# A hybrid decoder layer on one core: room of the output passes, issuer of the last stores, order of the last pair

## The chip, the cores and the metric

One core of a Trainium2 chip runs the whole layer in one launch. The metric is the device time of one execution in microseconds (us). Timed three times, the kernel before took 1909.26 us in the median (1907.34 to 1910.01). The engines are named as the profile names them: PE is TensorE (matmul), PEld its weight load, DVE is VectorE, ACT is ScalarE, POOL is GpSimd, and SP is the engine that issues DMA transfers; SPq is its queue.

## The reference

The layer has 2048 tokens of 1024 features, all float32. Cut to what matters:

```python
u = rmsnorm(h, norm_mix);  z = u @ w_in                    # 1024 -> 5392
aq, ak, av, gq, gk, gv, g_low, za, zg = split(z)
y_att = swa_sink_attention(rope(aq), rope(ak), av, sinks)  # 16 heads, window 128
log_g = log_sigmoid(g_low @ w_gate_up + b_gate) / 16
y_gla = rmsnorm(gla_chunked(gq, gk, gv, log_g), gla_norm)  # 4 heads
y = concat([y_att * silu(za), y_gla * silu(zg)]) @ w_out   # 2048 -> 1024
h = h + y
gate = sigmoid(rmsnorm(h, ple_norm) @ w_ple_gate)          # 1024 -> 1024
h = h + gate * (p @ w_ple_proj)                            # 256 -> 1024
out = rmsnorm(h, final_norm)
```

## The kernel before

Every float32 product is taken as three matmuls: each operand is split into a rounded part h (ScalarE copies it to float32r) and a rest l (VectorE or GpSimd subtracts), and hh + hl + lh are summed in PSUM.

**Phase 1** computes the input projection and both groups of heads, in two halves of eight token tiles. `uth` and `utl` hold the normed input of a half, transposed. `load_w` (L265 to L294) brings columns of w_in through `raw` tiles, splits them into wh and wl in one of two weight slots, and keeps the split form in DRAM for the second half. The results go to the DRAM tensors `yts`, one per token tile: features 0 to 7 by the attention tiles (L480), 8 to 15 by the four gated heads (`gla_tile`, store at L587). In the second half the generator `right_operands` also prepares the right-hand matrices of the output passes and stores them to DRAM (`td`). The key and value buffers and the raw tiles (`kvp`, `rawp`) lie at the right end of SBUF; they are closed before the gate weights of the last gated head are loaded, and the first three prepared matrices are loaded into their place (`tpr`).

**Phase 2** is three passes: pass 0 and 1 multiply the two halves of y by w_out and add the residual, pass 2 is the gate with w_ple_gate. Each works on pairs of token tiles, in blocks of one or two pairs: (0,1), (2), (3), (4), (5), (6,7), and in pass 2 (0,1), (2) to (7). A pair's 256 by 1024 times 1024 by 1024 product is formed by seven products of quarter blocks, by sums and differences of blocks (`combos` makes the left operands C, `T[i]` are the right ones). The seven are taken in ORDER = (0, 4, 1, 6, 5, 2, 3); each is 12 matmuls of 512 columns (`prod`, L774 to L776). Products 1, 2 and 3 add onto the PSUM banks of 0, 4 and 6, and `after` says what is done with each result. In pass 0 and 1 the quarters of the result are summed into the residual tiles q11 to q22; `norm_pair` then squares and scales them, and its transposes run in the next block (`posts`).

In pass 2 (`gate_block`) each quarter passes through `gated`: sigmoid, times the projection of p (`proj`, four groups of six matmuls, on w_ple_proj loaded by `load_wq`), plus the residual hr, and a square for the final norm; `finish` scales and stores to `out`. `load_p` brings a tile of p, transposes and splits it. For the last pair, product 3 is done in two halves of 256 columns (`halves`), and each of the other steps follows it.

**What sets the order.** The code is written in program order, but the order on each engine is laid down when the kernel is built, by a scheduler that simulates the instructions with estimated costs: of those that can run, the one that stands first in the program goes first. On the chip each engine then works strictly in that order; SP also issues its transfers in order, and each waits for its inputs and for a free buffer. Tiles with one tag share `bufs` buffers; a tile waits until its buffer's former tile has been read. With `reuse_waits="tile"` a tile of a new pool waits only for the older tiles at its own addresses.

The pools of phase 2 are laid from the left in the order in which they are opened: `xpb` (17 x2 tiles of 2 KiB, 8 C tiles of 4 KiB, 10 x2b tiles of 2 KiB), `tpb` (4 matrices of 16 KiB), `fs`. They lie over the weight slots (34 KiB), uth and utl (64), c1 and wk of phase 1. The weights of w_ple_proj (8 tiles) and of final_norm (2) are x2b tiles, of which the residuals of passes 0 and 1 (eight for a block of two pairs) also are. The gate pass takes its q tiles, p tiles and hr tiles from x2.

Of the kernel before, what the change touches and what calls it, by code (L numbers as in the profile page):

```python
# [38 lines left out]
def hybrid_block_kernel(  # L39
# [57 lines left out]
    def x2(name, shape=(P, 4, P), dtype=F32):  # L97
        return p2p["xpb"].tile(list(shape), dtype, name=name, tag="x2", bufs=17)
# [27 lines left out]
    with ExitStack() as p1:  # L126
        kvs = p1.enter_context(ExitStack())
        kvp = kvs.enter_context(tc.tile_pool(name="kvp", bufs=1, side="right"))
        rawp = kvs.enter_context(tc.tile_pool(name="rawp", bufs=9, side="right"))
# [39 lines left out]
        def constants():  # L169
# [33 lines left out]

            pos_f = wk.tile([16, P], F32, name="pos_f", tag="w1", bufs=8)
# [60 lines left out]
        def load_w(cols, fast=False):  # L265
# [9 lines left out]
            for k0 in range(0, KD, 2):  # L275
                ks_ = slice(k0, k0 + 2)
# [4 lines left out]
                raw = rawp.tile([P, 2, SW], F32, name="raw", tag="raw")  # L281
# [4 lines left out]
                act.activation(wh[:, ks_, 0:n], raw[:, :, 0:n], AF.Copy)  # L286
                eng = dve if fast and k0 % 4 == 0 else pool
                eng.tensor_tensor(wl[:, ks_, 0:n], raw[:, :, 0:n], wh[:, ks_, 0:n], op=ALU.subtract)  # L288
# [260 lines left out]
        def gla_tile(half, h, wz, lt, ops):  # L549
# [37 lines left out]
            pace[0] = nc.sync.dma_start(yts[t][:, 8 + 2 * h:10 + 2 * h, :], oy).ins  # L587
# [9 lines left out]
        def right_operands():  # L597
            units = [(ps_, k, c) for ps_ in range(3) for k in range(4) for c in range(4)]

            def piece(name, dtype=F32):  # L600
                return rawp.tile([P, 2 * SW], dtype, name=name, tag="raw")[:, 0:512].rearrange("p (b n) -> p b n", b=4)
# [54 lines left out]
        for half in range(2):  # L656
# [4 lines left out]
            for s_ in range(HT + LAG):  # L661
# [5 lines left out]
                if s_ < HT:  # L667
                    a = section_a(half, s_, wA)
                    next(a)
                    if half == 0 and s_ == 0:  # L670
                        constants()
                    tick()
# [11 lines left out]
            for i in range(4):  # L684
# [9 lines left out]
                if half == 1 and i == 3:  # L694
# [50 lines left out]
    with ExitStack() as p2:  # L745
        for name in ("xpb", "tpb", "fs"):
            p2p[name] = p2.enter_context(tc.tile_pool(name=name, bufs=1, reuse_waits="tile"))
        fs = p2p["fs"]
        load_T(0, ORDER[3:], T)


        def combos(As):
            Cs = [[None] * 7 for _ in As]
            ss = [x2("s1") for _ in As]
            for i in ORDER:
                for C, (a11, a12, a21, a22), s_ in zip(Cs, As, ss):
# [9 lines left out]
                    C[i] = p2p["xpb"].tile([P, 2, 4, P], F32R, name=f"c{i}", tag="c", bufs=8)  # L766
# [13 lines left out]
        def products(Cs, T, after, last=None):  # L780
            banks = [{} for _ in Cs]
            two = len(Cs) > 1
            for i in ORDER:
# [111 lines left out]
        def load_p(t):  # L895
            pi = x2("pi", (P, DPLE))
# [19 lines left out]
        def gate_block(prs, Cs, T, posts):  # L916
            two = len(prs) > 1
            last = prs[-1] == NP - 1
            qs = [[x2(f"q{i}", (P, 512)) for i in range(4)] for _ in prs]
# [11 lines left out]
            def finish(n, i, s2):  # L931
# [20 lines left out]
            def after(i, n, ps):  # L952
# [5 lines left out]
                elif i == 1:  # L958
                    act.activation(q11, ps, AF.Copy)
                elif i == 6:  # L960
                    add(dve, q22, q22, ps)
                elif i == 5:
                    add(dve, q21, q21, ps)
                    add(dve, q22, q22, q21)
                elif i == 2:
                    add(dve, q12, q21, ps)
                    s2 = sums()
                    pps = proj(pTs[n, 0], banks())
                    gated(n, 0, 0, pps, s2)
                    gated(n, 0, 1, pps, s2)  # L970
                    if last:
                        state["s"] = s2
                        state["p"] = proj(pTs[n, 1], [pt("t"), pt("t")])
                        state["s1"] = sums()
                        gated(n, 1, 1, state["p"], state["s1"])
                    else:
# [113 lines left out]
```

## Time and profile before

| | us |
|---|---|
| median of three runs (lowest, highest) | 1909.26 (1907.34, 1910.01) |
| the profiled execution | 1904.04 |
| its span, first to last instruction | 1902.3 |
| busy: TensorE matmul, weight load | 1814.7, 1612.9 |
| busy: VectorE, ScalarE, GpSimd | 1203.3, 961.1, 699.3 |

The span is what the profile shows of the profiled execution; 1.7 us lie around it. Busy times are sums over the span, so they say which engine could be the bound, and the windows say where. A matmul's start is measured and its end modelled, so the pace of TensorE is read from the distance of starts. The granted clock is given as a share of full speed: 1.0 is 2.4 GHz, 0.5 is 1.2 GHz. In a wait, the name behind the arrow is what ended it last.

### The profile page before, as it was taken

The numbers are of one execution on the slowest core, as the hardware profiler recorded it, in microseconds if no ns is written. First come the engines' busy times: TensorE is split into PE (matmuls) and PEld (weight loads), VectorE is DVE, ScalarE is ACT, GpSimd is POOL, SyncE is SP. The second block draws the span as 40 slices with busy tenths as digits, with TensorE's granted clock in tenths as the row PEclk, the third lists the DMA queues.
The fourth block names the chain that finished last, engine by engine and source line by source line (L and its number), as shares of the span: only waits on it lengthen the run. The fifth ranks groups of instructions, "written<-read, shape, count | busy, mean of one in ns | idle before, by whom it ended". The sixth has DMA issues, their size and how long they took to land. (4 is left out here: it accounts for less than half of the span.)

```text
span 1902.3 us, 32715 instructions
## 1 busy us (share of the span) xinstructions
PE 1814.7 (95%) x11297; PEld 1612.9 (85%) x11297; DVE 1203.3 (63%) x2663; ACT 961.1 (51%) x2598; POOL 699.3 (37%) x916
## 2 busy tenths in 40 slices
PE   6999999999999999999999999999899999998997
PEld 6989898998898889898888988988788888787886
DVE  6454785466556474578766756574667667665864
ACT  5544666465557464456654655563422244453543
POOL 5442554534526362544455445352200010102432
PEclk9999999999999999999999999999999999999998
DMA  8332442415324352655576566565685966884542
GB/s 281 122 101 81 147 136 92 155 53 170 97 66 143 102 180 90 199 146 174 178 205 206 163 195 182 160 195 192 230 281 194 324 237 219 313 309 151 179 139 83
DMA packets 326741, 326.78 MB, mean 172 GB/s; under 512 B 23137, under 2 KB 259825, under 8 KB 326321
## 3 DMA queue, kind: packets, MB, share of 16 engines
q1 hardware_dynamic: 326576, 324.70, 52.5%
q8 instruction: 89, 1.46, 0.3%
q14 instruction: 76, 0.61, 0.1%
HBM read 186.08 MB, written 138.54 MB: 171 GB/s over the span
## 5 line engine op out<-in xcount | busy, mean ns | idle before, releaser
L85 PE MATMUL acc<-wh,uth 128*128 128x256 f32 (+1 forms) x1664 | 476.8, 287 | 14.5 <-DVE m L563 4.5
L86 PE MATMUL acc<-wl,uth 128*128 128x256 f32 (+1 forms) x1664 | 472.6, 284 | 6.2 <-DMA wl<-wd 6.0
L87 PE MATMUL acc<-wh,utl 128*128 128x256 f32 (+1 forms) x1664 | 471.1, 283 | 0.0
L85 PEld LDWEIGHTS acc<-wh,uth 128*128 128x128 f32 x1664 | 316.0, 190 | 25.6 <-ACT v L522 5.9
L86 PEld LDWEIGHTS acc<-wl,uth 128*128 128x128 f32 x1664 | 315.7, 190 | 12.9 <-DMA wl<-wd 8.6
L87 PEld LDWEIGHTS acc<-wh,utl 128*128 128x128 f32 x1664 | 315.7, 190 | 2.0
L460 POOL TENSOR_TENSOR pq<-pq,pmask 128x512 fp32r<-128x512 f32 x128 | 178.2, 1408 | 292.9 <-ACT pq L67 285.8
L85 PE MATMUL acc<-uth,wh 128*128 128x512 f32 x512 | 204.3, 399 | 4.8 <-DVE m L563 3.8
L87 PE MATMUL acc<-uth,wl 128*128 128x512 f32 x512 | 201.7, 394 | 0.3 <-DMA wl<-wd 0.3
L86 PE MATMUL acc<-utl,wh 128*128 128x512 f32 x512 | 201.9, 394 | 0.0
L774 PE MATMUL acc<-T,c 128*128 128x512 f32 (+1 forms) x344 | 135.5, 395 | 6.7 <-ACT u L829 6.3
L775 PE MATMUL acc<-T,c 128*128 128x512 f32 (+1 forms) x344 | 135.1, 393 | 0.0
L776 PE MATMUL acc<-T,c 128*128 128x512 f32 (+1 forms) x344 | 135.0, 393 | 0.0
L446 ACT ACTIVATE s<-s,sm 128x128 f32<-128x128 f32 x256 | 99.7, 391 | 51.1 <-DVE sm L442 51.1
L85 PEld LDWEIGHTS acc<-uth,wh 128*128 128x128 f32 x512 | 96.4, 188 | 26.8 <-DVE m L563 5.2
L859 POOL TENSOR_TENSOR ssh<-ssh 128x1 f32<-128x1 f32 x16 | 3.3, 205 | 313.8 <-ACT junk L858 313.8
L288 POOL TENSOR_TENSOR wl<-raw,wh 128x512 fp32r<-128x512 f32 (+1 forms) x82 | 109.6, 1367 | 20.0 <-ACT wh L286 10.2
L87 PEld LDWEIGHTS acc<-uth,wl 128*128 128x128 f32 x512 | 96.1, 188 | 22.5 <-DMA wl<-wd 0.7
L86 PEld LDWEIGHTS acc<-utl,wh 128*128 128x128 f32 x512 | 96.2, 188 | 18.7
L67 ACT ACTIVATE c<-s 128x512 fp32r<-128x512 f32 x72 | 45.1, 629 | 111.1 <-DVE s L104 32.4
L774 PE MATMUL o<-T,c 128*128 128x512 f32 (+1 forms) x252 | 99.3, 394 | 0.0
L775 PE MATMUL o<-T,c 128*128 128x512 f32 (+1 forms) x252 | 98.6, 391 | 0.0
(289 smaller groups left out, 4409.7 us busy)
## 6 DMA issues: line engine op xcount, KB each, us to landing
T<-td SPq DMA_DIRECT2D x84, 512.0 KB, 9.4
wd<-wh SPq DMA_DIRECT2D x20, 1024.0 KB, 5.6
wd<-wl SPq DMA_DIRECT2D x20, 1024.0 KB, 6.3
wh<-wd SPq DMA_DIRECT2D x80, 256.0 KB, 5.4
wl<-wd SPq DMA_DIRECT2D x80, 256.0 KB, 5.5
raw<-in_w_in SPq DMA_DIRECT2D x68, 256.0 KB, 5.6
y<-yts SPq DMA_DIRECT2D x64, 256.0 KB, 5.6
td<-th SPq DMA_DIRECT2D x48, 256.0 KB, 2.8
```

The source lines that it names most:

```text
L67: act.activation(h, src, AF.Copy)
L85: pe.matmul(ps, lhs_h(k), rhs_h(k), start=(k == 0), stop=False)
L86: pe.matmul(ps, lhs_h(k), rhs_l(k), start=False, stop=False)
L87: pe.matmul(ps, lhs_l(k), rhs_h(k), start=False, stop=(k == nk - 1))
L288: eng.tensor_tensor(wl[:, ks_, 0:n], raw[:, :, 0:n], wh[:, ks_, 0:n], op=ALU.subtract)
L446: act.activation(s[:, j, :], s[:, j, :], AF.Exp, bias=ng[:, j:j + 1], accum_out=su[:, j:j + 1])
L460: pool.tensor_tensor(pq[:, 2 + i, :].rearrange("p (h n) -> p h n", h=4), pq[:, i, :].rearrange("p (h n) -> p h n", h=4), pmb, op=ALU.mult)
L774: pe.matmul(ps, c[:, 0, k, :], t[:, 0, k, sl], start=(first and k == 0), stop=False, skip_group_check=more)
L775: pe.matmul(ps, c[:, 0, k, :], t[:, 1, k, sl], start=False, stop=False, skip_group_check=more)
L776: pe.matmul(ps, c[:, 1, k, :], t[:, 0, k, sl], start=False, stop=(k == 3), skip_group_check=more)
L859: pool.tensor_tensor(ss[:, 0:1], ss[:, 0:1], ss[:, 1:2], op=ALU.add)
```

## The change

It has these parts.

1. Phase 2's pools are laid out anew. `tpr` holds two matrices instead of three, and beside it at the right end lies a new pool `xpa` with the x2 tiles, 15 instead of 17. On the left stand in this order `tpb` (5 matrices), `cpl` (the 8 C tiles), `xpb` (x2b only), `wqp` (w_ple_proj and final_norm, a buffer for each) and `fs`, with a buffer for a p tile.
2. The gate pass takes its q tiles from x2b. `load_wq` is called before the block of pair 3 in pass 1, not in the first block of pass 2. p tiles are asked for at the head of a gate block; in the block of two pairs hr is loaded after product 5 as before.
3. The eight yts stores of the last gated head in the second half are issued by ScalarE (`nc.scalar.dma_start`), and no longer set `pace`.
4. The last pair of pass 2 is taken in the order LAST = (0, 4, 6, 5, 1, 2, 3). Its four projections follow product 6, the quarters are gated after 5, 1 and 2, and the first tile is finished before the halves of product 3. Both tiles are scaled by VectorE.
5. `raw` tiles have 512 columns instead of 2 x 272, and there are ten instead of nine. The first load of the 272 columns for k, v and the gate takes one k at a time: 16 transfers instead of 8, and 8 splits instead of 4.
6. The rotary tables are a function of their own, called right behind `constants`.

```diff
     def x2(name, shape=(P, 4, P), dtype=F32):
-        return p2p["xpb"].tile(list(shape), dtype, name=name, tag="x2", bufs=17)
+        return p2p["xpa"].tile(list(shape), dtype, name=name, tag="x2", bufs=15)
...
-            T[i] = p2p["tpr" if i in ORDER[:3] else "tpb"].tile(
-                [P, 2, 4, 512], F32R, name=f"T{i}", tag="T", bufs=3 if i in ORDER[:3] else 4)
+            T[i] = p2p["tpr" if i in ORDER[:2] else "tpb"].tile(
+                [P, 2, 4, 512], F32R, name=f"T{i}", tag="T", bufs=2 if i in ORDER[:2] else 5)
...
-            for k0 in range(0, KD, 2):
-                ks_ = slice(k0, k0 + 2)
+            kn = 2 if n <= 256 or saved is not None else 1
+            for k0 in range(0, KD, kn):
+                ks_ = slice(k0, k0 + kn)
...
-                eng = dve if fast and k0 % 4 == 0 else pool
-                eng.tensor_tensor(wl[:, ks_, 0:n], raw[:, :, 0:n], wh[:, ks_, 0:n], op=ALU.subtract)
+                eng = dve if fast and k0 % (2 * kn) == 0 else pool
+                eng.tensor_tensor(wl[:, ks_, 0:n], raw, wh[:, ks_, 0:n], op=ALU.subtract)
...
-            pace[0] = nc.sync.dma_start(yts[t][:, 8 + 2 * h:10 + 2 * h, :], oy).ins
+            if half == 1 and h == 3:
+                nc.scalar.dma_start(yts[t][:, 8 + 2 * h:10 + 2 * h, :], oy)
+            else:
+                pace[0] = nc.sync.dma_start(yts[t][:, 8 + 2 * h:10 + 2 * h, :], oy).ins
...
-                    p2p["tpr"] = p2r.enter_context(tc.tile_pool(name="tpr", bufs=1, side="right", reuse_waits="tile"))
+                    for name in ("tpr", "xpa"):
+                        p2p[name] = p2r.enter_context(
+                            tc.tile_pool(name=name, bufs=1, side="right", reuse_waits="tile"))
                     T = [None] * 7
-                    load_T(0, ORDER[:3], T)
+                    load_T(0, ORDER[:2], T)
...
-        for name in ("xpb", "tpb", "fs"):
+        for name in ("tpb", "cpl", "xpb", "wqp", "fs"):
...
-            pi = x2("pi", (P, DPLE))
+            pi = fs.tile([P, DPLE], F32, name="pi", tag="pi", bufs=1)
...
-            qs = [[x2(f"q{i}", (P, 512)) for i in range(4)] for _ in prs]
+            qs = [[x2b(f"q{i}") for i in range(4)] for _ in prs]
...
-                    if last and not i:
-                        act.activation(o, o, AF.Copy, scale=rs2)
-                        pool.tensor_tensor(o, o, fn[j], op=ALU.mult)
-                    else:
-                        dve.scalar_tensor_tensor(o, o, rs2, fn[j], op0=ALU.mult, op1=ALU.mult)
+                    dve.scalar_tensor_tensor(o, o, rs2, fn[j], op0=ALU.mult, op1=ALU.mult)
...
                 elif i == 1:
                     act.activation(q11, ps, AF.Copy)
+                    if last:
+                        state["s0"] = sums()
+                        gated(n, 0, 0, state[0], state["s0"])
...
                     add(dve, q22, q22, q21)
+                    if last:
+                        state["s"] = sums()
+                        gated(n, 1, 1, state[1], state["s"])
...
+                    if last:
+                        gated(n, 0, 1, state[0], state["s0"])
+                        finish(n, 0, state["s0"])
...
-                    if not posts and two:
-                        load_wq()
-                if i == (5 if two else 6):
-                    for h in range(1 if two else 2):
-                        pTs[n, h] = load_p(2 * prs[n] + h)
-                        hrs[n, h] = load_r(2 * prs[n] + h)
+                if i == 5 and two:
+                    hrs[n, 0] = load_r(2 * prs[n])
...
+            if two:
+                for n in range(2):
+                    pTs[n, 0] = load_p(2 * prs[n])
+            else:
+                for h in range(2):
+                    pTs[0, h] = load_p(2 * prs[0] + h)
+                    hrs[0, h] = load_r(2 * prs[0] + h)
...
                 if i == 6:
                     state["b6"] = ps
+                    state[1] = proj(pTs[n, 1], [pt("t"), pt("t")])
+                    state[0] = proj(pTs[n, 0])
                 after(i, n, ps)
...
+        LAST = (0, 4, 6, 5, 1, 2, 3)
...
+            if ps_ == 1 and prs == (3,):
+                load_wq()
```

## Rows read from the trace of the kernel before

**Rows 1.** First lines of the page: the span, TensorE's busy time and matmuls.
```profile
span 1902.3 us, 32715 instructions
...
PE 1814.7 (95%) x11297; PEld 1612.9 (85%) x11297; DVE 1203.3 (63%) x2663; ACT 961.1 (51%) x2598; POOL 699.3 (37%) x916
```
**Rows 2.** Windows: length, busy PE, PEld, DVE, ACT, POOL (instructions), clock, DMA, GB/s.
```profile
0.00:50.00 50.00, 33.62 (x220) 31.40 (x221) 31.85 (x81) 29.45 (x65) 27.45 (x72) 0.92 0.83 273
...
1350.00:1400.00 50.00, 45.35 (x188) 36.51 (x189) 34.79 (x57) 15.96 (x30) 1.49 (x4) 0.93 1.01 354
...
1700.00:1750.00 50.00, 44.78 (x205) 35.92 (x204) 25.82 (x41) 17.66 (x34) 7.13 (x7) 0.97 0.39 133
...
1850.00:1900.00 50.00, 40.52 (x194) 33.63 (x192) 26.94 (x49) 18.03 (x43) 12.30 (x17) 0.93 0.25 85
```
**Rows 3.** Timeline of TensorE at the handover: start, duration, instruction, [idle before it, releaser].
```profile
1360.08 0.39 PE L776 MATMUL o<-T,c 128*128 128x512 f32 x1
...
1362.80 0.39 PE L776 MATMUL o<-T,c 128*128 128x512 f32 x1
1367.68 0.80 PE L774 MATMUL acc<-T,c 128*128 128x512 f32 x1 [4.50 <-ACT u L829]
...
1374.00 0.39 PE L774 MATMUL acc<-T,c 128*128 128x512 f32 x1
```
**Rows 4.** Timeline of SP at the handover, and its longest wait from 1290 to 1375.
```profile
1322.56 22.71 SPq L587 DMA_DIRECT2D yts<-oyg  x4
1345.36 3.63 SPq L805 DMA_DIRECT2D y<-yts  x5
...
1363.01 17.91 SPq L122 DMA_DIRECT2D T<-td  x16
...
SPq L587 <- ACT oyg L586: 21.1, 2, 15.4
```
**Rows 5.** Timeline of VectorE at the handover.
```profile
1357.29 0.69 DVE L107 TENSOR_TENSOR s<-y 128x512 f32<-128x512 f32 x1 [1.20 <-DMA y<-yts]
```
**Rows 6.** Timeline of SP in the first block of the gate pass.
```profile
1717.05 0.90 SPq L1032 DMA_DIRECT2D raw<-in_w_ple_proj  x2
...
1723.37 0.42 SPq L897 DMA_DIRECT2D pi<-in_p  x1
```
**Rows 7.** Timeline of TensorE behind these loads.
```profile
1727.66 0.41 PE L901 MATMUL t<-identr,pi 128*128 128x128 f32 x2 [4.09 <-DMA pi<-in_p]
...
1727.83 0.48 PE L774 MATMUL o<-T,c 128*128 128x512 f32 x1
...
1732.25 0.38 PE L901 MATMUL t<-identr,pi 128*128 128x128 f32 x2
```
**Rows 8.** Timeline of TensorE earlier in that block: i = 5, two of seven transposes (L870).
```profile
1698.36 0.39 PE L774 MATMUL acc<-T,c 128*128 128x512 f32 x1
...
1704.26 0.60 PE L870 MATMUL t<-identr,xt 128*128 128x128 f32 x4
...
1720.66 0.60 PE L870 MATMUL t<-identr,xt 128*128 128x128 f32 x4
```
**Rows 9.** Timeline of all engines at the end.
```profile
1885.56 0.42 DVE L107 TENSOR_TENSOR q<-q,o 128x256 f32<-128x256 f32 x1 [1.32 <-PE o L776]
...
1886.01 0.42 ACT L925 ACTIVATE q<-q 128x256 f32<-128x256 f32 x1 [1.33 <-DVE q L107]
...
1890.13 0.39 PE L913 MATMUL t<-wph,pT 128*128 128x512 f32 x1
...
1892.17 0.15 DVE L107 TENSOR_TENSOR s<-s 128x1 f32<-128x1 f32 x1
...
1895.95 1.00 DVE L107 TENSOR_TENSOR s<-s 128x1 f32<-128x1 f32 x1 [0.23 <-ACT junk L929]
```
**Rows 10.** Timeline of SP at the start, and TensorE's wait for kst, once, 5.3 us.
```profile
4.32 5.52 SPq L284 DMA_DIRECT2D raw<-in_w_in  x6
...
PE t L392 <- DVE kst L373: 5.3, 1, 5.3
```

More of the change, by code (lines that the diff above doesn't have):

```diff
@@ L128, in hybrid_block_kernel @@
         kvp = kvs.enter_context(tc.tile_pool(name="kvp", bufs=1, side="right"))
-        rawp = kvs.enter_context(tc.tile_pool(name="rawp", bufs=9, side="right"))
+        rawp = kvs.enter_context(tc.tile_pool(name="rawp", bufs=10, side="right"))
         wps = [p1.enter_context(tc.tile_pool(name=f"wp{i}", bufs=1)) for i in range(2)]
@@ L280, in load_w @@
                     continue
-                raw = rawp.tile([P, 2, SW], F32, name="raw", tag="raw")
+                raw = rawp.tile([P, 512], F32, name="raw", tag="raw")[:, 0:kn * n].rearrange("p (k n) -> p k n", k=kn)
                 o = 0
@@ L600, in piece @@
             def piece(name, dtype=F32):
-                return rawp.tile([P, 2 * SW], dtype, name=name, tag="raw")[:, 0:512].rearrange("p (b n) -> p b n", b=4)
+                return rawp.tile([P, 4, P], dtype, name=name, tag="raw")
             def load(ps_, k, c):
@@ L765, in combos @@
                     src = {0: a11, 4: s_, 1: a12, 6: a21, 5: s_, 2: s_, 3: a22}[i]
-                    C[i] = p2p["xpb"].tile([P, 2, 4, P], F32R, name=f"c{i}", tag="c", bufs=8)
+                    C[i] = p2p["cpl"].tile([P, 2, 4, P], F32R, name=f"c{i}", tag="c", bufs=8)
                     split(C[i][:, 0], C[i][:, 1], src)
@@ L776, in prod, with products @@
                 pe.matmul(ps, c[:, 1, k, :], t[:, 0, k, sl], start=False, stop=(k == 3), skip_group_check=more)
-        def products(Cs, T, after, last=None):
+        def products(Cs, T, after, last=None, order=ORDER):
             banks = [{} for _ in Cs]
             two = len(Cs) > 1
-            for i in ORDER:
+            for i in order:
                 if i == 6 and two:
@@ L1015, in after_last, with wqt @@
                     state["b6"] = ps
+                    state[1] = proj(pTs[n, 1], [pt("t"), pt("t")])
+                    state[0] = proj(pTs[n, 0])
                 after(i, n, ps)
-            products(Cs, T, after_last if last else after, halves if last else None)
+            if last:
+                products(Cs, T, after_last, halves, LAST)
+            else:
+                products(Cs, T, after)
         NP = NT // 2
+        LAST = (0, 4, 6, 5, 1, 2, 3)
         wq_, fn = [], []
+        def wqt(name, dtype=F32):
+            return p2p["wqp"].tile([P, 512], dtype, name=name, tag=name)
         def load_wq():
             for n, ns in enumerate(NS):
-                fn.append(x2b(f"fn{n}"))
+                fn.append(wqt(f"fn{n}"))
                 nc.sync.dma_start(fn[n], final_norm[ns].partition_broadcast(P))
@@ L1029, in load_wq @@
                 for ns in NS:
-                    hl = [x2b(f"wp{c}", dtype=F32R) for c in "hl"]
+                    hl = [wqt(f"wp{c}{k}{len(wq_[k])}", F32R) for c in "hl"]
                     raw = x2("raw3", (P, 512))
@@ L1040, in left @@
         def left(ps_, prs):
-            return combos([load_h(2 * pr) if ps_ == 2 else load_y(ps_, 2 * pr) for pr in prs])
+            return combos([load_h(2 * pr) if ps_ == 2 else load_y(ps_, 2 * pr) for pr in prs],
+                          LAST if ps_ == 2 and prs[-1] == NP - 1 else ORDER)
         def residual(ps_, prs):
```

29 lines of the change are left out of this document (13 added, 16 removed).

## The prediction

> **What bounds the kernel now.** I read the page first: TensorE is busy for 1814.7 of 1902.3 us [rows 1], so a change can only give back what lies in the remaining 88 us, or lengthen it. The windows of 50 us were next, to see where that is. Four of them bear on this change [rows 2]: the first (16.4 us idle, granted clock 0.92), 1350 to 1400 where phase 1 hands over to the output passes (4.7 us idle, clock 0.93), 1700 to 1750 where the gate pass begins (5.2 us, 0.97), and the last. Then the timelines of TensorE and of the DMA-issuing queue SP in those windows.
>
> At the handover TensorE stops after 1362.80 and starts its next product at 1367.68, noted as a wait of 4.50 us for ScalarE's copy u. It then goes at the lower of its two clock levels: from 1367.68 to 1374.00, 15 matmuls take 6.3 us, where 12 before the stop took 2.72 (1360.08 to 1362.80), so 0.227 each and 3.4 for 15 [rows 3]. That is 2.9 us more. Behind the copy stands a queue that began late: SP sits in the four stores of yts from 1322.56 to 1345.27, the next thing it issues are the loads of y at 1345.36, and VectorE still waits for such a load at 1357.29 [rows 4, 5]. SP's wait for oyg, which these stores need, is 21.1 us in two pieces [rows 4]. Loads that need nothing from this phase stand behind stores that do.
>
> In the gate pass the loads of w_ple_proj leave at 1717.05 and the first p load behind them at 1723.37 [rows 6]. TensorE waits 4.09 us for that p tile, and the 12 matmuls of the next product (1727.83 to 1732.25) take 4.42 us instead of 2.72, so 1.7 for the clock [rows 7].
>
> At the end the last matmul starts at 1890.13 and ends at 1890.52; the span ends at 1902.3 [rows 1, 9]: 11.8 us after TensorE.
>
> **The change part by part.** The profiled execution took 1904.04 us, the median of the three runs is 1909.26; differences are worked out in the profiled one and taken off the median.
>
> *Handover.* The loads of y get room (xpa, 15 tiles, 30 KiB) in the right-hand space, which the key/value buffers have left before the last heads' loop starts, and the eight last stores leave SP. So y can be on the chip, and the sums on VectorE done, before 1345. The splits into C still wait, as cpl lies (by the sizes of the pools in their order) over the end of utl and over c1, which are read until the last gemm near 1347. From there a product of 12 matmuls takes 2.7 us and an operation of that size on VectorE 0.69 [rows 5], so the splits stay ahead. The four products of i = 0 and 4 begin at about 1350.5 as now and last to about 1361. I take the whole wait, 4.5, and the clock, 2.9: 7.4 off. The bounds: 0, if another input is late at the same place; 7.6, if the window's other idle time, 0.2, goes too [rows 2]. What is late next is T: only two of seven matrices are loaded ahead instead of three. The third comes into the space of the weights of q and k, which are done before the last loop ends; four more wait for the last gemm. In the trace 16 loads, four matrices, are issued in 17.91 us [rows 4], 4.5 a matrix, against 5.4 us for the two products that use one. Begun at 1347 they keep ahead; I price this at 0.
>
> *Stores on ScalarE.* Eight more instructions on an engine that is busy for about half of that stretch. No DMA is issued there in the trace; the nearest row, SP's own, is 0.42 us for one [rows 6]. Eight on the path would be 3.4, none 0. Queued behind each are the split of the state and the next gate; I take 0.3, since only the last one stands before work that TensorE is short of. On this edit the row and a rule part ways. The row says that SP held the y loads for the length of a wait [rows 4]. The Trainium skill (DMA: Bandwidth & Descriptors, Issuing engines are not separate DMA queues) says that issuing from several engines saves only the time in which the sequencer initiates a DMA. By that sentence the y loads would come forward by eight issues only, 3 us, and the handover would give about 3; by the row it gives 7.4. I follow the row; the other result is a rival below.
>
> *Gate pass.* The eight tiles of w_ple_proj and the two of final_norm get a pool of their own and are loaded in pass 1, four blocks ahead of the one that uses them; the p tiles get a buffer in fs and are asked for at the head of the block. So both of SP's late items [rows 6] are gone: 4.1 and 1.7, 5.8 us off. Their four splits on ScalarE and VectorE move beside products of pass 1, where TensorE alone decides. The single p buffer makes the second p load wait for the transposes of the first on SP's queue, with hr, hT and the stores of out behind it; at most one landing of a p tile per pair, hidden by 8 us and more of products: 0. What is late next are the q tiles. They move to x2b, 10 buffers, of which eight still hold the residuals of the last block of pass 1; two are free, and the others are freed one by one by the transposes after the norm. The first product that depends on it is i = 5 at 1698.36, which needs the bank that the fifth q tile empties, so three releases. In the trace the third of the transposes is at 1704.26 and the last at 1720.66 [rows 8], but there nothing waits for them, and they give way to products. Bounds: 0 to 10 us (below); I take 0.
>
> *Last pair.* The 24 matmuls of the projection move from behind the last product to its sixth; TensorE ends when it did, but what follows is one quarter of the rows' work instead of four. New tail: behind a half product come VectorE's add (at 1885.56) and the sigmoid (at 1886.01), each 0.42 with 0.03 between [rows 9]; with three more steps of that size (multiply, add, square) and five such gaps 2.3 us. From the first of the last sums at 1895.95 to the end are 6.35 us, in which one sum took 1.00 instead of 0.15 [rows 9], because GpSimd, which then does the other tile's final scaling, no longer has any: two sums are 0.3. So 2.3 + 6.35 - 0.7 is 7.95, up to 8.7 without that saving. From 11.8: 3.1 to 3.8 off; I take 3.3. A tail as long as now, 0, is the lower bound.
>
> *Start.* The first weights come in eight pieces of one k instead of four of two: eight more DMAs in the first 12 us. Six of the present ones took 5.52 us to issue [rows 10], 0.92 each, so up to 7.4 us later for what is queued behind; but the bytes are the same, and the splits of half the length can start sooner. TensorE's largest stall of the start, 5.3 us for kst [rows 10], hangs on the rotary tables, whose chain on VectorE waits among others for the gate weights behind these loads; it is the bound on the other side, 5.3 earlier. I take 1.2 us slower, about the middle. Calling the tables apart from the constants changes no order: 0. The tenth raw buffer: 0.
>
> Sum: -7.4 + 0.3 - 5.8 - 3.3 + 1.2 = -15.0 us. 1904.04 becomes 1889.0, and the median 1894.3.
>
> **The rivals.**
> A. The handover gives nothing: the instructions are laid in order ahead of time, by costs, and ScalarE and VectorE work in that order; the copy u may again stand behind a split whose C buffer, one of 8 for 14, is not free. For it: the wait is named as one for ScalarE, not for a DMA [rows 3]. Against: VectorE's late y [rows 5]. Time 1894.3 + 7.4 = 1901.7.
> B. Stores on ScalarE save issue time only: 3 instead of 7.4, 1898.7. Against it: SP's wait of 21.1 us [rows 4].
> C. The q tiles wait where the transposes stand now: i = 5 starts after the third transpose (1704.26 + 0.60) and the copy (about 0.5) instead of at 1698.36, 7.1 us, and the lower clock after it, 2.9: 10.0, so 1904.3.
> D. Slower: the same place, but all eight residuals are freed last. From 1698.36 to 1720.66 and the transposes and copy after it are 23.4 us, with the clock 26.3: 1920.6. It decides from a wait of 12.1 us on, where gain and loss are equal (15.0 - 2.9). For it: 8 of 10 buffers are held. Against: the transposes stand spread from 1692 on.
> E. The start is later by the full eight issues: 7.4 instead of 1.2, 1900.5.
>
> **How the numbers follow.** About 0.2% of the time, 3.8 us, is what a measurement of this kernel can tell from no change. Forecast 0.54, with its own range of 1890 to 1899; A 0.14, B 0.08, C 0.09, D 0.06, E 0.09. A, B, E and the forecast are faster by over 3.8 us (below 1905.4), and three quarters of C: 0.87 after a deduction for two of them at once. Same 0.07, slower 0.06. Range: low 1886, where the start gains its 5.3 instead of losing 1.2 and the runs' own spread, 2.7, takes part of the rest; high 1905, which takes in A, B, C and E singly.
>
> **What would show it.** Right: y loads long before 1345, and no wait of over 1 us and no clock of 0.6 in the first 15 us of the output passes; no wait for pi in the gate pass; w_ple_proj loads in pass 1; about 8 us from TensorE's last matmul to the end, and no projection matmul among the last 24. Wrong: a wait at the first i = 1 product, for u or for T; a wait at i = 5 of the first gate block for a copy of q; kst later than 44.7 in the first window.

## The result, and the profile after

The changed kernel takes 1916.3 us in the median of six runs (1914.38 to 1920.98); the kernel before, run beside it, 1907.1 (1900.54 to 1910.01). The ratio is 1.0051, 95% interval 1.0034 to 1.0067: slower by 9 us, where 15 us faster was forecast, and outside the range. The profiled execution took 1914.67 us with a span of 1912.9.

The first lines of its page [rows 1 before]:

```profile
span 1912.9 us, 32691 instructions
...
PE 1817.8 (95%) x11297; PEld 1616.2 (84%) x11297; DVE 1211.6 (63%) x2667; ACT 959.7 (50%) x2600; POOL 697.1 (36%) x916
```

The four windows, columns as in [rows 2]:

```profile
0.00:50.00 50.00, 28.88 (x201) 27.04 (x201) 26.02 (x54) 24.70 (x56) 25.45 (x66) 0.94 0.86 273
1350.00:1400.00 50.00, 41.10 (x226) 35.05 (x226) 27.74 (x55) 18.23 (x49) 10.97 (x19) 0.93 0.77 280
1700.00:1750.00 50.00, 49.12 (x235) 40.57 (x234) 30.24 (x47) 26.84 (x49) 5.72 (x10) 1.00 0.80 290
1850.00:1900.00 50.00, 50.00 (x227) 41.31 (x226) 26.00 (x44) 18.71 (x42) 11.23 (x15) 1.00 0.18 61
```

TensorE has the same 11297 matmuls and is busy for 3 us more. In the first window it does 4.7 us less; the other three windows hold work that is 12 to 21 us earlier in the kernel than the same windows of before, so their busy times show stalls but can't be subtracted: there still is a hole at 1350 to 1400, and none worth the name at 1700 to 1750.

To place the difference I took, in both traces, the moment at which TensorE had started the same amount of its work (columns of matmuls). The changed kernel is behind by 8.1 us at 75 us, by 14.8 at 1350, by 17.6 at 1420, by 20.6 at 1710, by 12.6 at 1800 and 12.4 at its last matmul; the end behind that is 1.9 shorter. That is the spans' difference, 10.6 (rounded). All stage figures below are made so, from profiled executions, against the profile of before.

**Start.** Timeline of the changed kernel, several engines, in order of time:

```profile
4.05 8.67 SPq L287 DMA_DIRECT2D raw<-in_w_in  x14
...
22.95 11.16 SPq L287 DMA_DIRECT2D raw<-in_w_in  x13
...
34.67 3.26 SPq L193 DMA_DIRECT2D wu<-in_w_gate_up  x3
...
42.08 0.63 ACT L198 ACTIVATE wup<-wu 16x512 fp32r<-16x512 f32 x1 [6.26 <-DMA wu<-in_w_gate_up]
...
43.39 0.68 DVE L201 TENSOR_TENSOR wup<-wu,wu 16x512 fp32r<-16x512 f32 x1 [5.82 <-ACT wu L200]
...
52.70 0.34 PE L395 MATMUL t<-identr,kst 128*128 128x128 f32 x1 [11.21 <-DVE kst L376]
```

Read upwards: TensorE waits 11.21 us for kst, the split keys, instead of 5.3 [rows 10]; VectorE had the split of the gate weights (wu) in front of the rotary tables that kst needs; ScalarE's first copy of wu waited for its transfer; and that left SP at 34.67, behind 13 raw loads that took 0.86 us each. Before, it left at 26.50, which is 8.2 us earlier, the size of the loss:

```profile
26.50 3.34 SPq L193 DMA_DIRECT2D wu<-in_w_gate_up  x4
```

SP issues 33 raw loads ahead of wu now (2, 14, 3, 1 and 13) and issued 18 before (2, 6, 4, 5 and 1). Eight of the 15 more are the finer pieces; the last of the 16 pieces has been issued at 12.72, where the last of the eight had at 9.84, 2.9 us later. The other seven are loads of the next weights, 17 of which now stand ahead of wu instead of 10.

**Handover.** Timeline of the changed kernel:

```profile
1315.06 12.09 SPq L815 DMA_DIRECT2D y<-yts  x12
...
1342.98 37.57 SPq L122 DMA_DIRECT2D T<-td  x20
...
1374.55 4.38 ACTq L592 DMA_DIRECT2D yts<-oyg  x2
...
1379.03 0.63 ACT L67 ACTIVATE c<-s 128x512 fp32r<-128x512 f32 x1 [8.59 <-DMA T<-td]
...
1380.20 0.50 PE L784 MATMUL acc<-T,c 128*128 128x512 f32 x1 [0.92 <-ACT u L839]
...
1381.59 3.79 SPq L815 DMA_DIRECT2D y<-yts  x4
...
1387.24 6.15 SPq L824 DMA_DIRECT2D xt<-in_x  x10
...
1391.74 0.69 DVE L107 TENSOR_TENSOR s<-y 128x512 f32<-128x512 f32 x1 [2.20 <-DMA y<-yts]
...
1393.81 0.79 PE L784 MATMUL acc<-T,c 128*128 128x512 f32 x1 [6.29 <-DVE xt L107]
1394.41 0.63 PE L785 MATMUL acc<-T,c 128*128 128x512 f32 x1
...
1398.67 0.57 PE L786 MATMUL acc<-T,c 128*128 128x512 f32 x1
```

y is early, as predicted (1315 instead of 1345 [rows 4]), and the wait for u is 0.92 instead of 4.50 [rows 3]. In its place stands a wait of 6.29 us for xt, the residual: the x loads are issued at 1387, behind 20 T loads and four y loads (before, the first ten left between 1351 and 1363, ahead of 16 T loads), and VectorE's next sum of y, placed ahead of the residual's additions in its order, waits as well. Behind it 12 matmuls go at the lower clock level (0.43 apart instead of 0.227). ScalarE stands still for 8.59 us around two of its stores; the trace names a T load as what ended it. The first of the ten x loads before:

```profile
1351.27 2.02 SPq L814 DMA_DIRECT2D xt<-in_x  x3
```

What comes late is also a matter of bytes. Two windows of 5 us of the changed kernel, columns as in [rows 2]:

```profile
1350.00:1355.00 5.00, 5.00 (x45) 5.00 (x45) 2.57 (x8) 2.12 (x9) 2.27 (x6) 1.00 0.09 31
1375.00:1380.00 5.00, 4.28 (x20) 3.17 (x18) 0.30 (x1) 0.97 (x2) 0.00 (x0) 1.00 1.05 390
```

The DMA engines are all but idle until the room of phase 1 comes free and full from then on: the share is 1.02 to 1.06 from 1365 to 1395. The kernel before has the same picture earlier (0.00 from 1335 to 1345, about 1.0 from 1350 to 1400). In both, once they are full, one T load lands about every 1.36 us, so a matrix of four takes 5.4, as long as the two products that use one; the prediction's 4.5 was the pace of issuing.

**Gate pass.** Timeline of the changed kernel:

```profile
1600.52 3.58 SPq L1054 DMA_DIRECT2D raw<-in_w_ple_proj  x4
...
1717.15 0.38 PE L911 MATMUL t<-identr,pi 128*128 128x128 f32 x2
...
1718.84 0.63 PE L880 MATMUL t<-identr,xt 128*128 128x128 f32 x4 [0.88 <-ACT q L963]
```

No wait for a p tile is left [rows 7 before], and 0.88 for a copy q is the only one of the block. It gains 8.0 us. Pass 1, where w_ple_proj is now loaded, loses 3.0 (17.6 behind at 1420, 20.6 at 1710).

**End.** Timeline of the changed kernel:

```profile
1902.58 0.28 PE L786 MATMUL o<-T,c 128*128 128x256 f32 x1
...
1904.99 1.41 DVE L949 SCALAR_TENSOR_TENSOR q<-q,rms,fn 128x512 f32<-128x512 f32 x2
...
1906.32 0.42 DVE L107 TENSOR_TENSOR q<-q,hr 128x256 f32<-128x256 f32 x1
...
1907.37 0.16 DVE L107 TENSOR_TENSOR s<-s 128x1 f32<-128x1 f32 x1 [0.57 <-ACT junk L939]
...
1908.47 1.42 DVE L949 SCALAR_TENSOR_TENSOR q<-q,rms,fn 128x512 f32<-128x512 f32 x2 [0.94 <-POOL rms L73]
```

From the start of the last matmul to the end of the span are 10.3 us; before, 12.2 (1890.13 to 1902.3 [rows 1, 9]).

### The profile page after: what moved, and what is told of

Same layout as the page of the kernel before. It is cut to its first block, busy times and chain, and to the rows that moved or that the text cites. A ratio compares the mean times of both kernels' runs of the same rounds, so it can differ in the third digit from the quotient of the medians.

```text
span 1912.9 us, 32691 instructions
## 1 busy us (share of the span) xinstructions
PE 1817.8 (95%) x11297; PEld 1616.2 (84%) x11297; DVE 1211.6 (63%) x2667; ACT 959.7 (50%) x2600; POOL 697.1 (36%) x916
## 4 chain that ended last, share of the span: by engine, by line
PE 64%; DMA 11%; DVE 11%; ACT 9%; issue 2%; SPq 2%; POOL 1%; DVEq 0%; POOLq 0%; ACTq 0%
PE acc L85 12%; PE acc L86 11%; PE acc L87 11%; PE acc L784 3%; PE acc L785 3%; PE acc L786 3%; DMA y<-yts 2%; PE o L784 2%; PE o L785 2%; PE o L786 2%; DMA T<-td 2%; ACT s L449 2%; DMA wl<-wd 1%; PE s L432 1%; DMA wh<-wd 1%
## 5 line engine op out<-in xcount | busy, mean ns | idle before, releaser
L85 PE MATMUL acc<-wh,uth 128*128 128x256 f32 (+1 forms) x1664 | 476.4, 287 | 14.8 <-DVE m L566 4.4
```

The costliest lines, as they stand in the source:

```text
L85: pe.matmul(ps, lhs_h(k), rhs_h(k), start=(k == 0), stop=False)
```

## The experiments

Each was timed in five rounds beside the kernel before; the ratio is to that. `part 5` is the finer first load. The stage figures of all are gathered behind them.

**a_start_undone.** The changed kernel with load_w and raw as before:

```diff
-            kn = 2 if n <= 256 or saved is not None else 1
-            for k0 in range(0, KD, kn):
+            for k0 in range(0, KD, 2):
...
-        rawp = kvs.enter_context(tc.tile_pool(name="rawp", bufs=10, side="right"))
+        rawp = kvs.enter_context(tc.tile_pool(name="rawp", bufs=9, side="right"))
```

> The changed kernel with part 5 taken back (raw tiles of 2 x 272 columns, nine of them, the first weights in four pieces of two k). Theory: the +8.1 us that the changed kernel shows in the first 76 us come from part 5 alone (more and finer raw loads stand ahead of the gate weights on SP, so the kst wait is 11.2 instead of 5.3 us). Then the kst wait is 5 to 6 us again, TensorE's work at 76 us is where it was before, and the time falls by 8: about 1908. Rival: the start only sets how long later stages wait (the distance to the kernel before sinks from 9.6 to 8.2 us by 1140 us and rises again in the last third), so most of the 8 us is given back later: 1912 to 1916.

1903.99 us, ratio 0.9983 (0.9968 to 0.9997). The kst wait is 5.3 again and TensorE is 0.3 us behind at 75 us. The theory held for the start but not for the time: the ratio falls by 0.7%, about 13 us, where the theory had 8.

**b_start_only.** The kernel before with part 5 alone, the reverse of this diff.

> The kernel before with part 5 alone. Theory: +8 us, all of it in the first 76 us, with a kst wait near 11 us: about 1915 against 1907. Rival (my prediction's size): 1.2 us, kst wait 5 to 7, about 1908.

1921.63 us, ratio 1.0072 (1.0049 to 1.0095). 7.9 us at 75 us as expected, and 8.1 more by 1350, which neither theory had. Part 5 alone makes the kernel slower by at least as much as the whole change does (the intervals overlap).

**b_kn1.** The kernel before with the pieces of part 5 (`kn = 1` for the first columns), but nine raw tiles of the old size.

> The kernel before with the first 272 columns loaded one k at a time, but the raw tiles as they were, nine of 2 x 272 columns. Theory (number of pieces): +8 us at the start as in the whole of part 5, and none of the 8 us that part 5 added between 700 and 1340 us, which come from the tenth raw buffer or its size: about 1914. Rival (the tenth buffer lets more raw loads in front of wu): start unchanged, about 1906.

1918.84 us, ratio 1.0044 (1.0028 to 1.0061). The number of pieces holds nearly all of the start's loss: 6.4 of 7.9 us. The second half of the theory is undecided: the profile shows 6.6 us between 205 and 1350 without a tenth buffer, in a column that repeats to 4 us only (see below), while the ratio, 0.44% or 8.4 us, is what the theory said, and its interval overlaps that of b_start_only. Waits of TensorE from 0 to 110, and SP's row of wu:

```profile
PE t L393 <- DVE kst L374: 9.6, 1, 9.6
```
```profile
33.06 3.26 SPq L193 DMA_DIRECT2D wu<-in_w_gate_up  x3
```

**b_start_wu.** b_start_only with the gate weights' four loads first:

```diff
+        wu0 = w2("wu0")
+        for i in range(4):
+            nc.sync.dma_start(wu0[32 * i:32 * i + 16, :], w_gate_up)
         wA = load_w(A_COLS, True)
...
-            wu0 = w2("wu0")
-            for i in range(4):
-                nc.sync.dma_start(wu0[32 * i:32 * i + 16, :], w_gate_up)
```

> The kernel before with part 5, and the four loads of the gate weights (wu) issued ahead of the first columns of w_in. Theory: part 5 costs its 8 us at the start only because 13 more raw loads stand ahead of wu on SP, and VectorE's order has the rotary tables and kst behind the split of wu. Then the kst wait falls from 11 us to 5 or less and TensorE's work at 76 us is 0 to 6 us earlier than in the kernel before; what part 5 adds between 700 and 1340 us (8 us in its own run) stays: 1906 to 1914. Rival: the raw loads' own bytes or pieces hold kst: the wait stays at 11 and the time near 1921.

1908.76 us, ratio 0.9997 (0.9980 to 1.0013): the kernel is level with the one before. SP and TensorE at the start:

```profile
4.08 2.97 SPq L646 DMA_DIRECT2D wu<-in_w_gate_up  x4
...
45.51 0.25 PE L390 MATMUL t<-identr,kst 128*128 128x128 f32 x1 [0.49 <-DVE kst L371]
```

So it was wu's place on SP, not the pieces' bytes. What kst no longer costs, the x tiles of the first half partly do (12.1 us in four waits), so part 5 gains nothing even then. With the old raw loads an early wu puts TensorE 3.0 us ahead at 205 (a_best_wu, below); here it is 0.8 behind.

**a_stores_sp.** The changed kernel with all stores of L592 issued by SP (`pace[0] = nc.sync.dma_start(...)`).

> The changed kernel with the eight last yts stores issued by SP again. Theory: the handover's loss hangs on room, not on the issuer (the residual tiles now lie on the end of phase 1's room, so the x loads stand behind 20 T loads and the next y on SP; TensorE's one long wait, 6.3 us, is for xt). Then the wait for xt stays near 6 us, or the y loads fall behind the stores as before, and the time stays within 3 us: 1914 to 1919. Rival: ScalarE's store issues are the cause (it stands still for 8.6 us around the two that took 4.38 us, and 4.3 us around the last): then both waits of TensorE at the handover (0.9 for u, 6.3 for xt) and the lower clock after them, 2.4, go: about 1908.

1920.48 us, ratio 1.0070 (1.0050 to 1.0089). The rival fell: without ScalarE's stores the wait for xt is not gone but 10.6 us. SP's part of my theory was too weak as well: the four stores hold SP for 23 us again, and the third T, the last four y loads and x move back behind them. By their intervals the medians of the two kernels are not clearly apart. SP, then TensorE:

```profile
1340.16 23.04 SPq L591 DMA_DIRECT2D yts<-oyg  x4
1363.30 2.71 SPq L122 DMA_DIRECT2D T<-td  x5
...
1392.48 7.38 SPq L821 DMA_DIRECT2D xt<-in_x  x10
...
1400.04 0.80 PE L781 MATMUL acc<-T,c 128*128 128x512 f32 x1 [10.60 <-DVE xt L107]
```

The Trainium skill (DMA: Bandwidth & Descriptors, Issuing engines are not separate DMA queues) has issuing from several engines save only the time of initiating. The run differs: eight issues would be 3.4 us, but the third T starts 20 us earlier when ScalarE issues the stores (1342.98; 3 of the 20 are that this run is later by then), because SP doesn't stand in their waits. The handover, however, is only 3.1 us shorter for it (2.9 lost instead of 6.0).

**a_xpb_left.** The changed kernel with the pools of phase 2 in another order:

```diff
-        for name in ("tpb", "cpl", "xpb", "wqp", "fs"):
+        for name in ("cpl", "xpb", "tpb", "wqp", "fs"):
```

> The changed kernel with its left-hand pools in the order cpl, xpb, tpb, wqp, fs: the residual tiles lie where the weight slots and uth were, and the x loads go ahead of T on SP. Theory (room): the wait of 6.3 us for xt and the 2.4 us of lower clock after it go, T becomes the next thing (five matrices after the last gemm instead of four, 4.5 us each against 5.4 for the two products that use one: no wait): about 1908. Rival: T is late instead, at the first i = 1 product: no gain, 1914 to 1918. Rival: ScalarE's blocked issues are the cause, then u and xt waits stay: 1916.

1915.67 us, ratio 1.0045 (1.0028 to 1.0063): in the main the first rival. The wait for xt is gone, and T is late, in short waits at the pace of its landing (2.3 us in seven); one of 2.5 us at the first product, for VectorE's m of phase 1, comes with it. SP's order now has four y loads, which take 7.92 us as they wait for buffers, ahead of all five T. SP:

```profile
1363.09 4.65 SPq L824 DMA_DIRECT2D xt<-in_x  x10
1370.43 7.92 SPq L815 DMA_DIRECT2D y<-yts  x4
1378.45 21.84 SPq L122 DMA_DIRECT2D T<-td  x20
```

TensorE's waits, 1335 to 1420:

```profile
PE acc L784 <- DVE m L566: 2.5, 1, 2.5
PE acc L784 <- DMA T<-td: 1.2, 4, 0.5
PE sw L784 <- DMA T<-td: 1.1, 3, 0.5
```

**a_hand2.** a_start_undone with C first, then three T, x2b, two T, wqp, fs.

> The changed kernel with part 5 taken back, and the left-hand room in another order: C, three T matrices, the residual tiles x2b, the last two T matrices, wqp, fs. The x loads and the next y then stand ahead of the last two T matrices on SP, and the bytes in the stretch are the same. Theory (place in SP's order, set by room): the wait for xt (5.7 us) and about 2 us of lower clock after it go: the distance to the kernel before at 1420 us falls from 7.4 to about 0, the time from 1904 to about 1897. Rival (bandwidth: the DMA engines are full from the last gemm on, so whatever stands last is late): a wait for T of about the same size takes its place, 1902 to 1906.

1902.1 us, ratio 0.9956 (0.9941 to 0.9971). The wait for xt is gone and the handover 2.6 us shorter than in a_start_undone (-0.9 instead of 1.7), not 7: the wait for u, which had seemed cured, is back at 3.8. And the next block waits 2.7 for xt at 1455, with the clock after it 4.6, so by the stages all of it is given back (7.1 lost in pass 1 instead of 4.2), as the rival said, though with u and xt late and not T. The median is 0.3% below that of a_start_undone; in the profiles that distance lies before 1349, up to where every engine has the same order of instructions in both, so it is no gain of the room. The two waits stand in these two rows (1335 to 1420, then 1440 to 1500):

```profile
PE acc L783 <- ACT u L838: 3.8, 1, 3.8
...
PE acc L783 <- DVE xt L107: 2.7, 1, 2.7
```

**a_layout_old.** a_start_undone with the room of the kernel before (x2, here 15 tiles, C and x2b in `xpb` on the left, three T on the right) and the stores on SP.

> The changed kernel with part 5 taken back, its last stores on SP, and the room of the kernel before (15 x2 tiles, C and x2b in xpb on the left, three T on the right, four in tpb); gate pass, wqp and last pair as changed. Theory: the new room gains nothing at the handover, it trades the 4.5 us wait for u against a wait of about 6 for xt. Then the wait for u is back at 4 to 5, that for xt is gone, and the distance to the kernel before at 1420 us falls from 7.4 to 0 to 5; the gate pass keeps its 8 us: 1897 to 1902. Rival: the new room did gain and only the wait for xt spoils it: the handover gets longer by 4 and the time is 1908 or more.

1901.54 us, ratio 0.9960 (0.9948 to 0.9973). The wait for u is 5.2, that for xt gone, and the handover is 0.75 us shorter than in the kernel before, where the new room lost 1.7. The new room gains nothing; the theory held.

**a_layout_old_act.** The same with the stores on ScalarE.

> The kernel of the run a_layout_old (room of the kernel before, part 5 taken back) with the eight last stores issued by ScalarE: the issuer alone. Theory: SP is free 20 us earlier, but in this room the y loads come when the last head's buffers are read, so they gain little, and ScalarE stands still where its store waits for a T load to land; the wait for u goes from 5.2 to 2 to 7: 1899 to 1905. Rival (my prediction): y comes ahead of the stores, the wait for u and the lower clock after it go, 7 us: about 1894.

1896.99 us, ratio 0.9938 (0.9915 to 0.9961). The wait for u is 4.0, the handover 0.8 us shorter than with SP's stores: near the theory, not my prediction. From a_start_undone this kernel differs by the room alone: its handover is 3.3 us shorter (-1.6 instead of 1.7) and its ratio lower, with intervals that don't overlap, so the new room costs time. In the profiles most of the distance to a_layout_old lies before 1350, where this kernel is 0.8 behind the kernel before and a_layout_old 8.1; the limit on such readings is given below.

**b_p_early.** The kernel before with p asked for at the head of the gate block:

```diff
-                        pTs[n, h] = load_p(2 * prs[n] + h)
...
+            for n in range(len(prs)):
+                for h in range(1 if two else 2):
+                    pTs[n, h] = load_p(2 * prs[n] + h)
             state = {}
```

> The kernel before, p tiles asked for at the head of a gate block and nothing else; w_ple_proj stays where it was. Theory: the p request's place alone makes the 6 to 8 us that the changed kernel gains in the first gate block: no wait for pi, 1900 to 1903 against 1908. Rival: with the old room and the weights in x2b behind it, w_ple_proj is then late for the first projection, gain 0 to 3: 1905 to 1908.

1908.37 us, ratio 0.9999 (0.9984 to 1.0013): the rival. The wait for pi is gone, and one for w_ple_proj takes its place, since its loads leave later than before (1726 instead of 1717 [rows 6]):

```profile
1726.24 0.38 SPq L1034 DMA_DIRECT2D raw<-in_w_ple_proj  x1
...
1730.90 0.80 PE L911 MATMUL t<-wph,pT 128*128 128x512 f32 x1 [4.38 <-ACT wph L67]
```

**a_gate_undone.** a_start_undone with `load_wq()` back in the first gate block, its tiles still in `wqp`.

> The changed kernel with part 5 taken back and load_wq called in the first block of the gate pass again (into its own pool). It tells apart two reasons for the gate pass's 8 us. Theory (loads of w_ple_proj): the first projection waits for them or for their splits, 4 to 6 us are lost again in the first block, and the 4 us that the changed kernel loses in pass 1 near 1600 (splits of these weights on ScalarE and VectorE) are gained back: within 2 us of 1904. Rival (p asked for at the head of the block is enough): the gate pass keeps its 8, pass 1 gains 4: about 1900. Third: the gate pass loses 8 and pass 1 gains nothing: 1912.

1903.18 us, ratio 0.9967 (0.9954 to 0.9980). The gate block keeps its 8.2 us and pass 1 loses 1.0 instead of 4.2: the rival by its profile, though the median is not clearly below that of a_start_undone. The w_ple_proj loads leave at 1720.16, and no projection waits. So their move into pass 1 gained nothing and cost about 3. What does gain is p early together with the new buffers (q in x2b, weights in wqp); these two were not separated.

**a_mix.** a_layout_old with load_wq in the gate block, wu early, and the first tile of the last pair scaled by ScalarE and GpSimd as before.

> What the runs so far point to, together: part 5 taken back, room of the kernel before, last stores on SP, load_wq in the first gate block again, p asked for early and the last pair in the new order as changed, its first tile scaled by ScalarE and GpSimd as before, and the loads of the gate weights ahead of the first columns of w_in. From a_layout_old (1901.5): load_wq back 3, the scaling off VectorE 1 to 1.5 in the tail (from the last matmul to the end 8.5 instead of 9.9), the early gate weights 0 to 5: 1893 to 1897. Rival: the early gate weights only move the wait to the x tiles of the first half, as in b_start_wu: 1898.

1897.99 us, ratio 0.9939 (0.9918 to 0.9959). The end takes 10.9 us, longer than with VectorE's scaling (10.3), not 8.5: ScalarE's squares then stand behind its own scaling. That part of the theory fell, and the time is the rival's.

**a_best.** a_layout_old_act with load_wq in the gate block.

> The changed kernel with part 5 taken back, the room of the kernel before, load_wq in the first gate block again; ScalarE's stores, the p tiles' early request, the pool wqp and the last pair's order stay. From a_layout_old_act (1897.0): the 3 us that load_wq costs in pass 1 come off, the first gate block keeps its 8: about 1894. Rival: in the old room the weights are late as in b_p_early (wait for wph, 4.9 us) and the gate block loses what pass 1 gains: 1897 to 1900.

1898.72 us, ratio 0.9954 (0.9939 to 0.9970). Gate block -8.2, pass 1 0.3: no wait for wph. The median isn't below a_layout_old_act's: the rival's time without the rival's wait. In its profile 5.8 us are lost before 1350.

**a_best_wu.** a_best with wu early.

> The kernel of a_best with the loads of the gate weights ahead of the first columns of w_in. Theory: the kst wait of 5.3 us goes, and 2 us of it are left after the x tiles of the first half wait instead (as in a_mix at 205 us): about 2 us less than a_best. Rival: the order of phase 1 shifts and the gain is gone before 1340 us (a_mix stood 6 us behind the kernel before there, a_layout_old 8): no difference.

1895.56 us, ratio 0.9943 (0.9925 to 0.9960), 3 us of the start kept at 205 us. The intervals of a_best, a_mix, a_layout_old_act and this one overlap; all are about 0.5% faster than the kernel before and 1% faster than the changed one.

**a_tail_noscale.** a_best without the two final multiplications of the last pair's first tile.

> The kernel of a_best with the scaling of the last pair's first tile left out (its two final multiplications; those rows are stored unscaled). In the changed kernel these two, 1.41 us, stand in VectorE's order ahead of the last addition of the second tile. Theory (they are what my sum of the tail left out): from TensorE's last matmul to the end 8.9 instead of 10.3 us. Rival (the two halves of the quarter, 7 instructions on VectorE instead of the 3 that I counted, are the whole of it): 10.0 or more.

1898.48 us, ratio 0.9954 (0.9939 to 0.9969), as a_best: 1 us is less than these medians tell. In the profiles the end takes 9.2 us against 10.3 in a_best: near the theory, 1.1 of its 1.4. VectorE and its last sum, then:

```profile
1887.54 0.76 DVE L107 TENSOR_TENSOR q<-q,hr 128x256 f32<-128x256 f32 x2
...
1889.13 0.16 DVE L107 TENSOR_TENSOR s<-s 128x1 f32<-128x1 f32 x1 [0.38 <-ACT junk L938]
```

The stage figures, in us against the kernel before (the last column is from the last matmul's start to the end; 12.2 before):

| | to 205 | 205 to 1350 | 1350 to 1420 | 1420 to 1710 | 1710 to 1800 | end |
|---|---|---|---|---|---|---|
| changed | 8.1 | 6.7 | 2.9 | 3.0 | -8.0 | 10.3 |
| b_start_only | 7.8 | 8.1 | 0.2 | -0.9 | 1.9 | 12.7 |
| b_kn1 | 6.4 | 6.6 | -1.5 | 1.1 | 3.9 | 10.2 |
| b_start_wu | 0.8 | 4.0 | -1.4 | 0.8 | 1.0 | 10.8 |
| a_start_undone | 0.3 | 5.5 | 1.7 | 4.2 | -8.0 | 10.3 |
| a_stores_sp | 7.8 | 10.1 | 6.0 | 3.3 | -8.1 | 10.3 |
| a_xpb_left | 7.6 | 6.9 | 2.7 | 4.8 | -8.1 | 10.4 |
| a_hand2 | 0.0 | 0.9 | -0.9 | 7.1 | -7.8 | 10.3 |
| a_gate_undone | -0.7 | 3.5 | 2.3 | 1.0 | -8.2 | 10.3 |
| a_layout_old | 1.3 | 6.7 | -0.8 | 3.9 | -8.1 | 10.3 |
| a_layout_old_act | 0.2 | 0.6 | -1.6 | 2.6 | -8.1 | 10.3 |
| b_p_early | 0.2 | 3.0 | -1.5 | -0.3 | 5.3 | 10.4 |
| a_mix | -1.4 | 7.4 | -0.1 | 1.4 | -8.2 | 10.9 |
| a_best | 0.2 | 5.8 | 0.8 | 0.3 | -8.2 | 10.3 |
| a_best_wu | -3.0 | 2.1 | -1.4 | 1.2 | -8.2 | 10.3 |
| a_tail_noscale | 0.4 | 1.7 | -0.7 | 2.1 | -8.2 | 9.2 |

The gate block's gain repeats within 0.4 us from kernel to kernel, the start's loss with part 5 and wu behind it within 0.5 for three of four (b_kn1 has less). The column 205 to 1350 does not: a_best and a_tail_noscale have the same instructions in the same order there and differ by 4. No single figure of that column is a cause. All entries in it are positive, so the profiled execution of before was a good one there (its 1904.04 lies below its medians).

## Why the prediction was wrong

By the profiles the sum missed by 25.6 us (-15.0 forecast, 10.6 measured): 6.9 at the start, 10.0 at the handover with the stores, 3.0 in pass 1 and 1.4 at the end, less 2.2 more gained in the gate pass (all rounded). The remaining 6.7 lie between 205 and 1350, where the sum had no term. a_start_undone shows 5.5 there without part 5, so their cause stays open.

**The start** failed most, by the medians. I took 1.2 us, "about the middle" of bounds of -5.3 and 7.4; it was 8.1, rival E and a little more. I had the chain (kst, tables, gate weights behind these loads) and then averaged instead of following it: with more loads in one in-order queue, whatever stands behind them leaves later, and the only thing TensorE was waiting for stood behind them. That it came out near E's 7.4 is partly luck: E counted eight more issues of 0.92 us, but the finer pieces account for 2.9 us, and the rest of the 8.2 came with seven more loads of the next weights that the new order put ahead of wu, a step that neither E nor I had. By medians part 5 costs more still, 0.7% in two comparisons (b_start_only, and changed against a_start_undone). The 8 us account for 0.4%; with wu moved the kernel is level again (b_start_wu), which suggests that the rest hangs on the late start; how it grows before 1350, and whether the raw tiles' new size and number take part (b_kn1 has 0.44%), stays open.

**The handover** failed next: 7.4 us off was forecast, 2.9 us were lost. Its first step was right: y early, the wait for u nearly gone. The step that failed is "what is late next is T": the x loads were not in my sum at all. Their tiles had been laid where phase 1 works to its end, behind 20 T loads on SP. The price of T, 0 at 4.5 us a matrix, was wrong with it: a matrix lands in 5.4 us, so T builds no lead, and whatever is put ahead of it or behind it in the full stretch is late. Taking the cover away one transfer at a time (a_xpb_left, a_hand2, a_layout_old) brought T, u and xt as the next wait in turn; none of the rooms made the handover more than 1.6 us shorter than before. Rival A had the place (no gain), not the reason.

**Stores on ScalarE**, 0.3 us, were mis-sized in both directions. Freeing SP is worth 3.1 us at the handover in the new room and 0.8 in the old, so B's 3 us is nearer than my 7.4. But they aren't free for ScalarE: 8.59 us of standing still. The trace shows why: the transfers of both engines count on the same eight semaphores in turn, and these two stores left at 1374.55 and 1378.61, less than 0.1 us after the T load that had used the same semaphore before had landed (1374.47 and 1378.53). TensorE lost 0.92 for u by it.

**The gate pass** came out near its size: -5.8 forecast, -8.0 in the block and 3.0 back in pass 1. The reason was half right. The late p was the wait, but loading w_ple_proj in pass 1, which I credited and priced at nothing, is where the 3 us went; b_p_early shows that p alone only hands the wait on. C and D were wrong: i = 5 did not wait.

**The last pair** gave 1.9 of the 3.3 us. From the last sum to the end it was 5.5 us, as worked out (6.35 - 0.7); the 2.3 us before it were 4.8. I counted one half's steps; the other half's stand between them on VectorE, and so do the two multiplications of the first tile, worth 1.1 (a_tail_noscale). Nor is the new order what shortened it: with the old one b_p_early ends in 10.4 and b_kn1 in 10.2, as there the projection's matmuls came to stand ahead of the last half product.

## What to carry to other kernels

- Where a queue is in order, price a finer load by who stands behind it: list what the queue issues up to the transfer that the bottleneck engine waits for, in the order of the changed kernel, as a new order can put other loads ahead too. If the wait for it is the one stall of the stage, there is no middle to take.
- When room is laid out anew, list every tile class that moves, and for each when its new place comes free and what then stands ahead of its load. A wait removed at a stage change is worth only the distance to the next wait; here three inputs took turns at being last.
- A transfer moved to a compute engine frees the queue that it left, and makes its new engine stand in the transfer's waits.

## What was not expected of the hardware

Two profiled executions with one order of instructions there drifted by 3.4 us inside one window (the first stands 0.4 us behind the second at its start and 3.8 at its end). The windows from 1250 to 1300 of a_best and of a_tail_noscale, columns as in [rows 2]:

```profile
1250.00:1300.00 50.00, 45.54 (x298) 41.61 (x299) 30.63 (x67) 26.88 (x74) 18.97 (x14) 0.93 0.58 173
```
```profile
1250.00:1300.00 50.00, 46.69 (x320) 42.30 (x321) 30.34 (x66) 26.19 (x72) 18.97 (x14) 1.00 0.63 189
```

Between 1210 and 1350 TensorE waits for weight loads (wl, wh) for 3.4 us in the first and 1.5 in the second; in the first the granted clock also falls, to a mean of 0.93, with 22 matmuls fewer in the window. So loads that land a microsecond or two later cost twice here. It bounds what one profile of such a kernel tells of a stage: 4 us where loads land just in time, half a microsecond where the same wait always ends last, as in the gate block.
